# A decoder trunk's mixer: projections dealt in four rounds, gates, then output projections; convolution, rotation and merge read PSUM; a smaller DMA scratch

## Chip, cores and metric

The kernel runs on one core of a Trainium2 chip. The metric is the device time of one execution in microseconds (us), here the median of three runs. TensorE (PE in the profile) does matrix products and writes them to PSUM, which has eight banks of 512 fp32 columns here; VectorE (DVE), ScalarE (ACT) and GpSimd (POOL) do the elementwise work, ACT with its function tables; SyncE (SP) issues the transfers from HBM. Every engine runs its own instructions in a fixed order and waits at semaphores for the others.

## The reference, cut to the mixer

Two layers, each a mixer, a mixture of experts and a per-layer embedding. 512 tokens, width 1024, fp32. The change touches the mixer:

```python
h = _rms_norm(x, norm_mix[i])
z = h @ w_in[i]                                  # 1024 -> 512*5 + 2*1024
q, k, v, cu, cg, ga, gb = jnp.split(z, W_IN_SPLITS, axis=-1)
q = _rope(q.reshape(B, S, N_HEADS, HEAD_DIM))    # 8 heads of 64
k = _rope(k.reshape(B, S, N_HEADS, HEAD_DIM))
v = v.reshape(B, S, N_HEADS, HEAD_DIM)
y_a = _dilated_mixture_attention(q, k, v) @ w_attn_out[i]
# causal depthwise convolution of 31 taps over u = cu * sigmoid(cg), then LayerNorm, silu
y_b = _conformer_conv(cu, cg, w_dw[i], b_dw[i], ln_conv_g[i], ln_conv_b[i]) \
    @ w_conv_out[i] + b_conv_out[i]
merged = jax.nn.sigmoid(ga) * y_a + jax.nn.sigmoid(gb) * y_b
x = x + merged @ w_out[i]
h2 = _rms_norm(x, norm_ffn[i])
x = x + _hier_moe(h2, ...)                       # 32 experts, 2 per token
g_ple = jax.nn.sigmoid(_rms_norm(x, norm_ple[i]) @ w_ple_gate[i])
x = x + g_ple * (p[i] @ w_ple_proj[i])
```

## The kernel before

**Weights and products.** The dense weights come in chunks of 512 KB, in the order of `SEQ_CHUNKS`. `load_chunks` (L207) issues a chunk's transfer on SP, `split_chunks` has ACT round it to `hi` (L225) and POOL form the rest `lo` (L230). A product then takes three passes (`mm3`, L288 to L290). `step_a` makes one tile of z transposed: a chunk of 128 columns against all 512 tokens, 8 x 3 = 24 matmuls into one PSUM bank (`ps_z`). Such a product is called a step here. The chunk names say what a step makes: `cu`, `cg` convolution value and gate (4 each), `q`, `k` (4 pairs of heads), `ga`, `gb` gates of the two branches (8 each), so 32 steps per layer. `v` (values) comes ahead of them in another layout, `ao` are the output projections of both branches, 24 matmuls for each of 8 column tiles (`ps_ya`, `ps_yb`), `wo` the product behind the merge (`ps_wo`).

**Order of a mixer before.** `v`; then four pairs `cu`, `cg`; then four pairs `q`, `k`; then three pairs of gates; then the `ao` projections, with the other five pairs of gates behind the first five of them. All steps write PSUM; ACT or DVE takes the result out. For the convolution DVE writes u = (tanh + 1) * value to SBUF (L514).

**Side work.** Everything that the steps feed lies in three queues: `conv` (the taps, two at a time), `attn` (rotation, and for each pair of heads six score groups with their softmax, transposes and the product with the values), `side` (the last taps of a chunk, LayerNorm and silu). A step calls `adv` four times; each call takes one entry from `conv` and `side`, and in the `q`, `k` and gate steps three from `attn`. So the place in which an entry is written follows from the steps; Tile's scheduler then fixes each engine's order, with `attn` and `side` at high priority.

**Taps.** 31 shifted multiply-adds per chunk (`tap`, L499: acc = u shifted * weight + acc). DVE does 26 of them, ACT with POOL the last five (`ptap`, L505, L506), by the table `KP`.

**Rotation.** ACT copies the product to `raw` (L677) and, in four pieces with the halves of each head exchanged, to `sw` (L679); DVE multiplies by cosine (L588) and sine (L589) and adds (L590) to `s_qk`. The scores (`ps_S`, L603) are PE's; DVE takes minimum and bias (L609), ACT the exponential (L611), DVE the reciprocal and scaling (L621, L625), PE the transposes (`ps_PT`, L637), and `ps_O` (L663) multiplies by the values.

**Memory.** SBUF tiles of 128 x 1024 come from a pool `s4` of 44, tiles of 128 x 512 from `s2` of 12. Expert weights take what `s4` has free (`pump`, L241).

Of the kernel before, what the change touches and what calls it, by code (L numbers as in the profile page):

```python
# [13 lines left out]
OP = mybir.AluOpType  # L14
# [16 lines left out]
# columns of the constant array  # L31
# [5 lines left out]
# columns of the per-layer array of small weights  # L37
# [29 lines left out]
AD = 3, 3, 3  # L67
KP = 5, 5, 5, 5
# [3 lines left out]
RP = "vvv"  # L72
# [6 lines left out]
N4, N2 = 44, 12  # L79


class Pinned:
    """An engine that issues its instructions in the order they are written."""
# [25 lines left out]
class Halved:  # L109
    """n rows of 512 columns, in halves of 256, four to a tile."""  # L110
# [15 lines left out]
class Slots:  # L126
    """Tiles of one size; a slot is free again once its last use is written down."""
# [15 lines left out]
class Rows:  # L143
    """n rows of 512 columns, two to a tile."""
# [11 lines left out]
class Trunk:  # L156
    def __init__(self, ctx, tc, x, pT, wd, wg, wu, wdn, sm, gains, cst, out):
# [16 lines left out]
        self.queues = []  # L174
        # expert weights in the order of their use
# [34 lines left out]
    def split_chunks(self, upto):  # L210
        """The parts of the weights that one pass carries each: rounded, and the rest."""
# [34 lines left out]
    def late_items(self):  # L246
        """Some of the first weights in use come last, into half tiles."""
# [53 lines left out]
    def step_a(self, c, adv=1):  # L301
        """A tile of z^T: a chunk of 128 columns against all tokens."""
# [3 lines left out]
        for k in range(KD):  # L306
            w = slice(k * P, (k + 1) * P)
            self.mm3(ps, ch[:, w], cl[:, w], hh(k), hl(k), k == 0, k == KD - 1)
            if k % 2:
                self.adv(adv)  # L310
# [3 lines left out]
    def step_b(self, c, acc, src, k0, first, last):  # L314
        """Token-layout products: a chunk of 2 x 128 rows against 512 columns."""
        ch, cl = self.take(c)
        for t in range(NT):
# [4 lines left out]
            self.adv(1)  # L322
# [34 lines left out]
    def squares(self, t, junk, h):  # L357
        """Sum of the squares of a half of a token tile."""
# [29 lines left out]
    def split_T(self, t, n, dst):  # L388
        """Transposes of one token tile into the two parts of dst."""
# [14 lines left out]
    def prep(self, t, gain, r, n):  # L404
        """RMSNorm(x) of a token tile."""
# [60 lines left out]
    def mixer(self, l):  # L466
# [9 lines left out]
        # values, in token layout  # L476
# [24 lines left out]
        def ptap(j, s):  # L501
            o, i = acc(j, s), u(j, 0, T - s)
# [6 lines left out]
        for j in range(4):  # L509
            pcu = self.step_a(pos[f"cu{j}"])  # L510
# [3 lines left out]
            v.scalar_tensor_tensor(u(j), th, 1.0, pcu, op0=OP.add, op1=OP.mult)  # L514
# [45 lines left out]
        def silu_part(j):  # L560
# [12 lines left out]
            if j == 3:  # L573
                self.s2.free()  # 1/std
# [11 lines left out]
        def rope(dst, raw, sw):  # L586
            e = [dict(p=nc.gpsimd, v=v)[a] for a in RP]
            e[0].tensor_tensor(dst, raw, self.cc(C_COS, T), op=OP.mult)  # L588
            e[1].tensor_tensor(sw, sw, self.cc(C_SIN, T), op=OP.mult)  # L589
            e[2].tensor_tensor(dst, dst, sw, op=OP.add)  # L590
# [80 lines left out]
        for p in range(4):  # L671
            st["qk", p] = Rows(self.s4, 2, what="qk")
            for i, nm in enumerate(("q", "k")):
                ps = self.step_a(pos[f"{nm}{p}"], adv=AD[0])
                raw, sw = self.s2.get(F32, "raw"), self.s2.get(F32, "sw")
                scale = 0.125 if nm == "q" else 1.0
                act.activation(raw, ps, AF.Copy, scale=scale)  # L677
                for b in range(0, P, 32):
                    act.activation(sw[b:b + 32], ps[b ^ 32:(b ^ 32) + 32], AF.Copy, scale=scale)  # L679
                self.ps.free()  # L680
                attn.append(lambda d=st["qk", p](i), r=raw, w=sw: rope(d, r, w))
# [3 lines left out]
            attn += [dict(u=us, t=tr, n=nm_)[a[0]][int(a[1])] if a != "-" else None for a in ATT.split()]  # L685
# [12 lines left out]
        gates = {}

        def gate(nm, j):  # L700
            ps = self.step_a(pos[f"{nm}{j}"], adv=AD[1])
            g = self.s2.get(F32, nm)
            act.activation(g, ps, AF.Tanh, scale=0.5)
            self.ps.free()
            gates[nm, j] = g

        for j in range(3):
            gate("ga", j)
            gate("gb", j)
        for q in self.queues:  # L710
            self.drain(q)
        self.look, self.ahead = LK[1], 1
        mT = Halved(self.s4, KD, F32R, "mTh"), Halved(self.s4, KD, F32R, "mTl")
        for j in range(8):
# [3 lines left out]
            for s, src in ((0, oT), (1, cv)):  # L718
# [4 lines left out]
            ga, gb = gates.pop(("ga", j)), gates.pop(("gb", j))  # L723
            yb = self.s2.get(F32, "yb")
            v.scalar_tensor_tensor(ga, ga, 1.0, pab[0], op0=OP.add, op1=OP.mult)
            act.activation(yb, pab[1], AF.Identity, bias=self.smt[:, S_BO + j:S_BO + j + 1])
            v.scalar_tensor_tensor(gb, gb, 1.0, yb, op0=OP.add, op1=OP.mult)
            v.tensor_add(ga, ga, gb)
            for h in range(2):
                a = slice(256 * h, 256 * h + 256)  # L730
                act.activation(mT[0].half(j, h), ga[:, a], AF.Copy, scale=0.5)
# [739 lines left out]
```

## Time and profile before

| | before |
|---|---|
| median of three runs | 2046.5 us (2046.15 to 2046.57) |
| span of the profiled execution, first to last instruction | 2042.4 us |
| PE busy | 1885.1 us |
| DVE busy | 984.4 us |
| ACT busy | 580.8 us |
| POOL busy | 419.5 us |
| mean granted clock of PE | 0.966 |

No time of its own is recorded for the profiled execution; its span is 4.1 us below the median. The page cuts the span into 40 slices and gives each engine's busy share in tenths. Further views are asked of the same trace: windows (busy time by stretch), waits (who waited for whom), single tiles, groups of instructions by line, and the timeline. Matmuls overlap in the pipeline, so the time of one (0.39 us) is longer than the distance between two.

### The profile page before, as it was taken

What the parts mean: (1) busy time and instruction counts of PE and PEld (TensorE: products, weight loads), DVE (VectorE), ACT (ScalarE), POOL (GpSimd) and SP (SyncE); (2) the same over time, 40 slices, a digit from 0 to 9 for tenths busy, and PEclk for the clock granted to TensorE, in tenths of its full rate; (3) what the DMA queues carried; (4) which work ended last, traced back from release to release, by engine and by line L of the source; (5) the groups of instructions that cost most, each with busy time, mean ns of one, the idle gap of its engine ahead of it and who ended that gap; (6) DMA issues with size and microseconds to landing.
All of it is one profiled execution on the core that took longest, in us unless ns stands there. A gap on an engine that the chain in (4) does not pass through costs nothing. (4 is left out here: it accounts for less than half of the span.)

```text
span 2042.4 us, 23393 instructions
## 1 busy us (share of the span) xinstructions
PE 1885.1 (92%) x8532; PEld 1120.8 (55%) x8532; DVE 984.4 (48%) x2171; ACT 580.8 (28%) x1097; POOL 419.5 (21%) x211
## 2 busy tenths in 40 slices
PE   6948999999999998999989589999999999989998
PEld 5835588854444344444777356888544444444446
DVE  5799751462333223223659997325532332233246
ACT  4235542321110112111634354423211111111135
POOL 4443452401000001000435353424010000000011
PEclk9978999999999999999999789999999999999999
DMA  5201133579999699896231012254899996999941
GB/s 215 70 31 42 42 124 121 198 268 371 390 395 409 261 409 399 321 347 272 86 109 64 32 32 72 93 194 147 315 371 381 409 408 264 409 356 349 362 193 42
DMA packets 133319, 478.59 MB, mean 234 GB/s; under 512 B 14800, under 2 KB 15312, under 8 KB 133200
## 3 DMA queue, kind: packets, MB, share of 16 engines
q1 hardware_dynamic: 133200, 477.04, 62.2%
q8 instruction: 70, 1.15, 0.2%
q14 instruction: 49, 0.40, 0.1%
HBM read 474.89 MB, written 2.10 MB: 234 GB/s over the span
## 5 line engine op out<-in xcount | busy, mean ns | idle before, releaser
L230 POOL TENSOR_TENSOR s_lo<-s_raw,s_hi 128x1024 fp32r<-128x1024 f32 x114 | 290.6, 2565 | 766.1 <-ACT s_hi L225 411.7
L1021 PE MATMUL ps_u<-s_w,s_xg 128*64 128x512 f32 x1024 | 266.8, 596 | 0.0
L1021 PE MATMUL ps_g<-s_w,s_xg 128*64 128x512 f32 x1024 | 241.9, 607 | 6.9 <-DVEq L1206 6.5
L1051 PE MATMUL ps_y<-s_w,s_hT 128*64 128x512 f32 x1024 | 241.1, 595 | 1.4 <-ACT s_hT L1040 1.4
L290 PE MATMUL ps_z<-s_hTh,s_lo 128*128 128x512 f32 x512 | 205.5, 401 | 1.2 <-POOL s_lo L230 1.2
L289 PE MATMUL ps_z<-s_hTl,s_hi 128*128 128x512 f32 x512 | 205.4, 401 | 0.0
L288 PE MATMUL ps_z<-s_hTh,s_hi 128*128 128x512 f32 x512 | 205.1, 400 | 0.0
L499 DVE SCALAR_TENSOR_TENSOR s_acc<-s_u,smt,s_acc 128x503 f32<-128x503 f32 (+17 forms) x200 | 203.2, 1038 | 2.1
L1030 DVE SCALAR_TENSOR_TENSOR s_h<-s_h,ps_g 128x512 f32<-128x512 f32 x32 | 21.9, 686 | 292.9 <-ACT s_h L1029 292.9
L1021 PEld LDWEIGHTS ps_u<-s_w,s_xg 128*64 128x64 f32 x1024 | 78.5, 137 | 144.0 <-issue 136.1
L1051 PEld LDWEIGHTS ps_y<-s_w,s_hT 128*64 128x64 f32 x1024 | 77.2, 137 | 146.3 <-issue 129.2
L1074 DVE TENSOR_TENSOR s_x<-s_x,ps_c 128x512 f32<-128x512 f32 x144 | 95.3, 684 | 128.0 <-PE ps_c L1071 127.2
L897 PE MATMUL ps_xg<-s_OH,s_xh 128*128 128x256 f32 x512 | 138.7, 306 | 19.7 <-ACT s_xg L993 17.6
L1040 ACT ACTIVATE s_hT<-ps_hT 128x512 f32<-128x512 f32 x32 | 19.1, 597 | 415.8 <-PE ps_hT L1038 368.3
L1021 PEld LDWEIGHTS ps_g<-s_w,s_xg 128*64 128x64 f32 x1024 | 69.5, 137 | 123.0 <-issue 75.7
L897 PE MATMUL ps_xg<-s_OH,s_xl 128*128 128x256 f32 x512 | 132.7, 292 | 0.0
L897 PEld LDWEIGHTS ps_xg<-s_OH,s_xh 128*128 128x128 f32 x512 | 99.3, 195 | 56.8 <-ACT s_xg L993 38.1
L225 ACT ACTIVATE s_hi<-s_raw 128x1024 fp32r<-128x1024 f32 x120 | 123.3, 1052 | 4.0 <-POOL s_lo L230 3.5
L1138 POOL TENSOR_TENSOR s_pTl<-s_pT,s_pTh 128x1024 fp32r<-128x1024 f32 x2 | 4.7, 2368 | 532.3 <-ACT s_pTh L1137 266.3
L897 PEld LDWEIGHTS ps_xg<-s_OH,s_xl 128*128 128x128 f32 x512 | 99.6, 195 | 22.8 <-issue 22.7
L290 PEld LDWEIGHTS ps_z<-s_hTh,s_lo 128*128 128x128 f32 x512 | 98.4, 192 | 24.8 <-issue 3.5
L289 PEld LDWEIGHTS ps_z<-s_hTl,s_hi 128*128 128x128 f32 x512 | 98.7, 193 | 24.1 <-issue 3.9
(250 smaller groups left out, 2928.3 us busy)
## 6 DMA issues: line engine op xcount, KB each, us to landing
s_w<-wu SPq DMA_DIRECT2D x256, 512.0 KB, 9.5
s_w<-wdn SPq DMA_DIRECT2D x256, 512.0 KB, 10.2
s_w<-wg SPq DMA_DIRECT2D x248, 512.0 KB, 10.1
s_raw<-wd SPq DMA_DIRECT2D x124, 512.0 KB, 3.5
s_w<-wg SPq DMA_DIRECT2D x16, 256.0 KB, 7.5
s_x<-x SPq DMA_DIRECT2D x4, 512.0 KB, 9.1
out<-s_n SPq DMA_DIRECT2D x8, 256.0 KB, 2.0
s_gain<-gains SPq DMA_DIRECT2D x3, 512.0 KB, 3.8
```

The source lines that it names most:

```text
L225: nc.scalar.activation(hi, raw, AF.Copy)
L230: nc.gpsimd.tensor_tensor(lo, raw, hi.bitcast(F32), op=OP.subtract)
L288: mm(out, lh, rh, start=start, stop=False)
L289: mm(out, lh, rl, start=False, stop=False)
L290: mm(out, ll, rh, start=False, stop=stop)
L499: v.scalar_tensor_tensor(o, i, w, o, op0=OP.mult, op1=OP.add)
L897: self.nc.tensor.matmul(ps, self.nh[o][t][:, k * P:(k + 1) * P], oh[:, t * GS:(t + 1) * GS], start=t == 0 and o == 0, stop=t == NT - 1 and ...
L1021: pe.matmul(ps[64 * e:64 * e + 64], xg[h // 2][:, s:s + CAP], self.half_item((l, w, 2 * p + e, h), k), start=h == 0 and k == 0, stop=h == ...
L1030: v.scalar_tensor_tensor(t, t, 1.0, pg, op0=OP.add, op1=OP.mult)
L1040: act.activation(o, ps, AF.Copy)
L1051: pe.matmul(ps[n][64 * e:64 * e + 64], h_[:, f * P + e * CAP:f * P + (e + 1) * CAP], self.item_tile[l, "d", 2 * p + e, f][:, n * T:(n + 1) ...
L1074: v.tensor_add(xs, xs, ps)
```

## The change

The chunks, and with them the steps, are dealt in four rounds: each round p is `cu`, `cg`, `q`, `k`, `ga`, `gb` of number p. After the rounds come the other four pairs of gates, and then all eight `ao` projections in a row. `adv` now runs `attn` at one entry per call, and at two in every fourth (`AD`). The gated value u stays in the PSUM bank of its product, and the taps read it there; the fourth chunk's 31 taps are all DVE's (`KP`). The rotation multiplies the product in PSUM: sine first, ACT exchanges the halves from SBUF, then cosine in PSUM and the sum (the sign of the sine table moves with it). The merge of the branches is done in the PSUM banks of the two projections, convolution first. All gates lie in `s4`, and their tiles are held until the merge. The scratch that is set aside for dynamic DMA is 4096 bytes per partition, and `s4` has 47 tiles. Comments are removed, which moves the line numbers.

```diff
-SEQ_CHUNKS = (["v0", "v1", "v2", "v3", "cu0", "cg0", "cu1", "cg1", "cu2", "cg2", "cu3", "cg3",
-               "q0", "k0", "q1", "k1", "q2", "k2", "q3", "k3",
-               "ga0", "gb0", "ga1", "gb1", "ga2", "gb2"]
-              + [s for j in range(8) for s in ([f"ao{j}"] + ([f"ga{j + 3}", f"gb{j + 3}"] if j + 3 < 8 else []))]
+SEQ_CHUNKS = ([f"v{i}" for i in range(4)]
+              + [f"{n}{p}" for p in range(4) for n in ("cu", "cg", "q", "k", "ga", "gb")]
+              + [f"{n}{j}" for j in range(4, 8) for n in ("ga", "gb")]
+              + [f"ao{j}" for j in range(8)]
...
-AD = 3, 3, 3
-KP = 5, 5, 5, 5
+AD = 1, 1, 1, 2
+KP = 5, 5, 5, 0
...
-N4, N2 = 44, 12
+N4, N2 = 47, 12
+SCRATCH = 4096
...
-    def adv(self, n=1):
+    def adv(self):
+        self.adv_n += 1
         for i, q in enumerate(self.queues):
-            for _ in range(n if i == 1 else 1):
+            for _ in range(AD[self.adv_n % len(AD)] if i == 1 else 1):
...
         def tap(j, s):
-            o, i = acc(j, s), u(j, 0, T - s)
+            o, i = acc(j, s), u[j][:, :T - s]
...
-        for j in range(4):
-            pcu = self.step_a(pos[f"cu{j}"])
+        def conv_in(j):
+            u[j] = pcu = self.step_a(pos[f"cu{j}"])
             pcg = self.step_a(pos[f"cg{j}"])
             th = self.s2.get(F32, "th")
             act.activation(th, pcg, AF.Tanh, scale=0.5)
-            v.scalar_tensor_tensor(u(j), th, 1.0, pcu, op0=OP.add, op1=OP.mult)
-            self.ps.free(2)
+            v.scalar_tensor_tensor(pcu, th, 1.0, pcu, op0=OP.add, op1=OP.mult)
+            self.ps.free()
...
-        def rope(dst, raw, sw):
-            e = [dict(p=nc.gpsimd, v=v)[a] for a in RP]
-            e[0].tensor_tensor(dst, raw, self.cc(C_COS, T), op=OP.mult)
-            e[1].tensor_tensor(sw, sw, self.cc(C_SIN, T), op=OP.mult)
-            e[2].tensor_tensor(dst, dst, sw, op=OP.add)
+        def rope(dst, ps, scale):
+
+            a, sw = self.s2.get(F32, "raw"), self.s2.get(F32, "sw")
+            v.tensor_tensor(a, ps, self.cc(C_SIN, T), op=OP.mult)
+            for b in range(0, P, 32):
+                act.activation(sw[b:b + 32], a[b ^ 32:(b ^ 32) + 32], AF.Copy, scale=scale)
+            v.scalar_tensor_tensor(ps, ps, scale, self.cc(C_COS, T), op0=OP.mult, op1=OP.mult)
+            v.tensor_tensor(dst, ps, sw, op=OP.add)
...
-        for p in range(4):
+        def pair(p):
             st["qk", p] = Rows(self.s4, 2, what="qk")
             for i, nm in enumerate(("q", "k")):
-                ps = self.step_a(pos[f"{nm}{p}"], adv=AD[0])
...
-                attn.append(lambda d=st["qk", p](i), r=raw, w=sw: rope(d, r, w))
+                ps = self.step_a(pos[f"{nm}{p}"])
+                with self.tc.high_priority(HP):
+                    rope(st["qk", p](i), ps, 0.125 if nm == "q" else 1.0)
...
+        for p in range(4):
+            conv_in(p)
+            pair(p)
+            gate_pair(p)
+            if p == 3:
+                conv.append(norm)
         self.scale_router()
...
+        for j in range(4, 8):
+            gate_pair(j)
+        for s in self.hT:
+            s.free()
         for q in self.queues:
             self.drain(q)
...
-            for s, src in ((0, oT), (1, cv)):
+            for s, src in ((1, cv), (0, oT)):
...
-            ga, gb = gates.pop(("ga", j)), gates.pop(("gb", j))
-            yb = self.s2.get(F32, "yb")
-            v.scalar_tensor_tensor(ga, ga, 1.0, pab[0], op0=OP.add, op1=OP.mult)
-            act.activation(yb, pab[1], AF.Identity, bias=self.smt[:, S_BO + j:S_BO + j + 1])
-            v.scalar_tensor_tensor(gb, gb, 1.0, yb, op0=OP.add, op1=OP.mult)
-            v.tensor_add(ga, ga, gb)
+            g = gates.pop(0)
+            ga, gb = g[:, :T], g[:, T:]
+            act.activation(pab[1], pab[1], AF.Identity, bias=self.smt[:, S_BO + j:S_BO + j + 1])
+            v.scalar_tensor_tensor(gb, gb, 1.0, pab[1], op0=OP.add, op1=OP.mult)
+            v.scalar_tensor_tensor(pab[0], ga, 1.0, pab[0], op0=OP.add, op1=OP.mult)
+            v.tensor_tensor(pab[0], pab[0], gb, op=OP.add)
...
-            if j + 3 < 8:
-                gate("ga", j + 3)
-                gate("gb", j + 3)
...
-    nc = bacc.Bacc("TRN2", target_bir_lowering=False, num_devices=1)
+    nc = bacc.Bacc("TRN2", target_bir_lowering=False, num_devices=1, dynamic_dma_scratch_size=SCRATCH)
```

How this moves the instructions is seen at two places. First PE's order in layer 0 where the first scores stand. Before, it is behind eleven whole steps (`ps_z_841` is `q1`, the eleventh, `ps_z_924` is `k1`; `s_qk_734` holds the first pair's rotated queries and keys):

```order
L289 MATMUL ps_z_841<-s_hTl_107,s_hi_634 128x512
L290 MATMUL ps_z_841<-s_hTh_103,s_lo_635 128x512
L603 MATMUL ps_S_875<-s_qk_734 128x128
L603 MATMUL ps_S_902<-s_qk_734 128x384
L603 MATMUL ps_S_875<-s_qk_734 128x256
L288 MATMUL ps_z_924<-s_hTh_100,s_hi_685 128x512
```

Now it is behind five steps and the first matmul of the sixth (`ps_z_580` is `ga0`, `ps_z_620` is `gb0`; `s_qk_476` holds the first pair):

```order
L290 MATMUL ps_z_580<-s_hTl_107,s_hi_411 128x512
L291 MATMUL ps_z_580<-s_hTh_103,s_lo_412 128x512
L289 MATMUL ps_z_620<-s_hTh_100,s_hi_442 128x512
L609 MATMUL ps_S_635<-s_qk_476 128x128
L609 MATMUL ps_S_663<-s_qk_476 128x384
L609 MATMUL ps_S_635<-s_qk_476 128x256
L290 MATMUL ps_z_620<-s_hTl_104,s_hi_442 128x512
```

The scores have moved ahead of six steps; a later score group now stands at the end of each step, where before several stood in one. Second, DVE's order at the first pair's rotation. Before, the rotation follows all 26 taps of the first two chunks (`s_u_405` holds chunks 0 and 1, `s_u_406` chunks 2 and 3, `s_acc` the sums; `s_c` are the tables):

```order
L499 SCALAR_TENSOR_TENSOR s_acc_407<-s_u_405,smt,s_acc_407 128x488
L499 SCALAR_TENSOR_TENSOR s_acc_407<-s_u_405,smt,s_acc_407 128x487
L589 TENSOR_TENSOR s_sw_773<-s_sw_773,s_c_94 128x512
L497 TENSOR_SCALAR s_acc_408<-s_u_406,smt 128x512
L588 TENSOR_TENSOR s_qk_734<-s_raw_772,s_c_93 128x512
L499 SCALAR_TENSOR_TENSOR s_acc_408<-s_u_406,smt,s_acc_408 128x511
L588 TENSOR_TENSOR s_qk_734<-s_raw_827,s_c_93 128x512
L590 TENSOR_TENSOR s_qk_734<-s_qk_734,s_sw_773 128x512
```

Now it stands among the taps of chunk 0, which read the bank `ps_z_417` (`cu0`); `ps_z_531` is `k0`, and the last row is the first score group's minimum:

```order
L501 SCALAR_TENSOR_TENSOR s_acc_405<-ps_z_417,smt,s_acc_405 128x503
L591 TENSOR_TENSOR s_raw_564<-ps_z_531,s_c_94 128x512
L594 SCALAR_TENSOR_TENSOR ps_z_531<-ps_z_531,s_c_93 128x512
L501 SCALAR_TENSOR_TENSOR s_acc_405<-ps_z_417,smt,s_acc_405 128x502
L501 SCALAR_TENSOR_TENSOR s_acc_405<-ps_z_417,smt,s_acc_405 128x501
L501 SCALAR_TENSOR_TENSOR s_acc_405<-ps_z_417,smt,s_acc_405 128x500
L595 TENSOR_TENSOR s_qk_476<-ps_z_531,s_sw_565 128x512
L501 SCALAR_TENSOR_TENSOR s_acc_405<-ps_z_417,smt,s_acc_405 128x499
L501 SCALAR_TENSOR_TENSOR s_acc_405<-ps_z_417,smt,s_acc_405 128x498
L501 SCALAR_TENSOR_TENSOR s_acc_405<-ps_z_417,smt,s_acc_405 128x497
L615 ISA s_S_636,m_639<-ps_S_635,s_c_93 128x128
```

Ahead of the first pair's last rotation instruction stand 14 convolution instructions now, where there were 52 taps and more; three further taps follow before the first minimum.

More of the change, by code (lines that the diff above doesn't have):

```diff
@@ L71 @@
 NRM = "vvv"
-RP = "vvv"
 AH = 4
@@ L173, in __init__ @@
         self.loaded = self.split_n = 0
-        self.queues = []
+        self.queues, self.adv_n = [], 0
         self.items, self.item_tile, self.item_next, self.ring = [], {}, 0, 0
@@ L309, in step_a @@
             if k % 2:
-                self.adv(adv)
+                self.adv()
         self.done(c)
@@ L488, in mixer @@
         self.scale_small(l)
-        u, acc = Rows(self.s4, 4, what="u"), Rows(self.s4, 4, what="acc")
+        acc = Rows(self.s4, 4, what="acc")
+        u = {}
         def tap(j, s):
-            o, i = acc(j, s), u(j, 0, T - s)
+            o, i = acc(j, s), u[j][:, :T - s]
             w = self.wh[:, j * CK + CK - 1 - s:j * CK + CK - s]
@@ L536, in mean_part @@
             nc.tensor.matmul(pm, self.cc(C_ONE, P), sums[0], start=True, stop=True)
-            self.s2.free()
+            sq = sums[0]
             for j in range(4):
                 v.tensor_sub(acc(j), acc(j), pm)
-                act.activation(u(j), acc(j), AF.Square)
+                t = sq if j == 0 else self.s2.get(F32, "sq")
+                act.activation(t, acc(j), AF.Square)
                 if j:
-                    v.tensor_add(u(0), u(0), u(j))
+                    v.tensor_add(sq, sq, t)
+                    self.s2.free()
             self.ps.free()
@@ L548, in var_part @@
             pv = self.ps.get(F32, "var")
-            nc.tensor.matmul(pv, self.cc(C_ONE, P), u(0), start=True, stop=True)
+            nc.tensor.matmul(pv, self.cc(C_ONE, P), sums[0], start=True, stop=True)
             a, y, t = (self.s2.get(F32, "ln") for _ in range(3))
@@ L684, in mixer @@
             tr = [lambda p=p, q=q: trans(p, q) for q in range(6)]
-            attn += [dict(u=us, t=tr, n=nm_)[a[0]][int(a[1])] if a != "-" else None for a in ATT.split()]
+            attn.extend(dict(u=us, t=tr, n=nm_)[a[0]][int(a[1])] if a != "-" else None for a in ATT.split())
             def last(p=p):
@@ L693, in mixer, with gate_pair @@
             attn.append(last)
-        self.scale_router()
[L698 to L709, printed above, removed]
+        gates = []
+        def gate_pair(j):
+            g = self.s4.get(F32, "g")
+            for i, nm in enumerate(("ga", "gb")):
+                ps = self.step_a(pos[f"{nm}{j}"])
+                act.activation(g[:, i * T:(i + 1) * T], ps, AF.Tanh, scale=0.5)
+                self.ps.free()
+            gates.append(g)
+        for p in range(4):
[4 more added lines that the diff above has]
+                conv.append(norm)
+        self.scale_router()
+        for j in range(4, 8):
+            gate_pair(j)
+        for s in self.hT:
+            s.free()
         for q in self.queues:
@@ L722, in mixer @@
             self.done(c)
[L723 to L728 removed]
+            g = gates.pop(0)
[4 more added lines that the diff above has]
+            v.tensor_tensor(pab[0], pab[0], gb, op=OP.add)
             for h in range(2):
                 a = slice(256 * h, 256 * h + 256)
[L731 to L732 removed]
+                act.activation(mT[0].half(j, h), pab[0][:, a], AF.Copy, scale=0.5)
+                v.scalar_tensor_tensor(mT[1].half(j, h), pab[0][:, a], 0.5, mT[0].half(j, h).bitcast(F32),
                                        op0=OP.mult, op1=OP.subtract)
             self.ps.free(2)
[L735 to L741 removed]
+            self.s4.free()
             self.pump(RING[0])
@@ L1398, in constants @@
     c[:, C_COS:C_COS + T] = np.cos(ang.astype(np.float64))
-    c[:, C_SIN:C_SIN + T] = np.sin(ang.astype(np.float64)) * np.where(i % HD < HD // 2, -1.0, 1.0)[:, None]
+    c[:, C_SIN:C_SIN + T] = np.sin(ang.astype(np.float64)) * np.where(i % HD < HD // 2, 1.0, -1.0)[:, None]
     c[:, C_BASE:C_BASE + 32] = np.arange(32) * CAP
```

25 lines of the change are left out of this document (6 added, 19 removed).

## The prediction

> **What bounds the kernel now.** I read the page first, for the engine whose share is highest and for where it has holes.
>
> ```profile
> PE 1885.1 (92%) x8532; PEld 1120.8 (55%) x8532; DVE 984.4 (48%) x2171; ACT 580.8 (28%) x1097; POOL 419.5 (21%) x211
> PE   6948999999999998999989589999999999989998
> DVE  5799751462333223223659997325532332233246
> ```
>
> TensorE (PE) is busy for 92% of the span. Each slice is 51 us; PE's digits drop to 4 in slice 3 and to 5 in slice 23, once in each layer, and exactly there VectorE (DVE) stands at 9. These are the mixers, the stages that the change rewrites. Next the windows view, cut at the mixer's first input product, at the hole, and at the first output projection (columns: stretch and its length, busy PE, weight loads, DVE, ACT, POOL, then PE's granted clock, DMA share and GB/s).
>
> ```profile
> 50.00:110.04 60.04, 60.03 (x265) 49.36 (x263) 47.49 (x47) 23.02 (x34) 30.94 (x13) 1.00 0.20 63
> 110.04:135.20 25.16, 0.00 (x1) 0.00 (x1) 24.91 (x23) 0.53 (x1) 15.19 (x9) 0.58 0.16 59
> 135.20:267.30 132.10, 121.76 (x476) 77.03 (x477) 113.19 (x238) 72.58 (x163) 44.96 (x30) 0.92 0.15 48
> 267.30:366.30 99.00, 98.43 (x435) 81.11 (x434) 30.64 (x47) 34.24 (x53) 36.48 (x15) 1.00 0.41 142
> 50.00:267.30 217.30, 181.80 (x741) 126.39 (x740) 185.60 (x306) 96.13 (x197) 91.09 (x51) 0.91 0.16 54
> 1058.80:1277.60 218.80, 183.35 (x742) 127.42 (x741) 184.85 (x306) 97.33 (x198) 93.06 (x51) 0.90 0.16 53
> ```
>
> PE stands still for 25 us while DVE works without a pause, and it loses 35.5 us of 217.3 in all; layer 1 repeats this. From 267.3 to 366.3 it is the other way round: PE is full and DVE has 30.6 us of work in 99. So the mixer is bound by DVE first and by PE later. The waits of PE name what it waited for (sum, times, longest): layer 0, then layer 1.
>
> ```profile
> PE ps_S L603 <- DVE s_qk L590: 27.1, 2, 25.2
> PE ps_PT L637 <- DVE den L621: 4.7, 2, 4.4
> PE ps_PT L637 <- DVE s_S L625: 3.5, 4, 1.8
> PE ps_S L603 <- DVE s_qk L590: 27.7, 3, 25.1
> ```
>
> The first scores wait for the rotation of the first pair, which stands in DVE's order behind the 52 convolution taps of two chunks (the order excerpts above). The 16 gate products, which wait for nothing of DVE's, come too late to fill the hole.
>
> **What PE alone would need.** First matmuls of the mixer and of the stage behind it, both layers, and the pitch of an input product:
>
> ```profile
> L288 PE MATMUL ps_z<-s_hTh,s_hi x256: 387/389/793, 50.0 to 349.3; 128*128 128x512 f32 x128
> L288 PE MATMUL ps_wo<-s_hi,s_mTh x32: 389/389/389, 366.3 to 387.3; 128*128 128x512 f32 x32
> L288 PE MATMUL ps_z<-s_hTh,s_hi x256: 387/389/793, 1058.9 to 1359.5; 128*128 128x512 f32 x128
> L288 PE MATMUL ps_wo<-s_hi,s_mTh x32: 389/389/390, 1376.5 to 1397.5; 128*128 128x512 f32 x32
> 50.03 0.39 PE L288 MATMUL ps_z<-s_hTh,s_hi 128*128 128x512 f32 x1
> 81.77 0.39 PE L290 MATMUL ps_z<-s_hTh,s_lo 128*128 128x512 f32 x1
> ```
>
> The mixer from cu0 to wo0 takes 316.3 us in layer 0 and 317.6 in layer 1. The last two rows are the first and the 141st matmul of an unbroken run: 31.74 / 140 = 0.2267 us each. A step (24 matmuls) is 5.44 us; 32 input steps are 174.1 us and 8 output projections 43.5 us. The attention's own matmuls, layer 0 (scores, transposes, values; only the second number is read), and the same six score matmuls at two clocks:
>
> ```profile
> 50.00:267.30 217.30, 26.97 (x64) 10.68 (x64) 14.73 (x32) 0.91 0.16 54
> 50.00:267.30 217.30, 18.72 (x80) 9.80 (x80) 5.31 (x16) 9.97 (x32) 0.91 0.16 54
> 50.00:267.30 217.30, 13.89 (x64) 6.31 (x64) 2.74 (x4) 2.39 (x4) 0.91 0.16 54
> 135.20 2.92 PE L603 MATMUL ps_S<-s_qk 64*128 64x128 f32 x6 [25.16 <-DVE s_qk L590]
> 166.20 1.56 PE L603 MATMUL ps_S<-s_qk 64*128 64x128 f32 x6
> ```
>
> They sum to 59.6 us with two small matmuls (about 2) to come, but part of it ran slowly: after the hole the six took 2.92 us against 1.56 later. The clock was 0.92 over 132.1 us, some 10 us of full speed missing, not all of it in these rows. So attention costs PE between 51 and 62 us; I take 54. PE's floor is 174.1 + 43.5 + 54 = 271.6 us, and what can be won is 316.3 - 271.6 = 44.7 and 317.6 - 271.6 = 46.0, together **90.7 us**. Cross-check: 35.5 of idle time plus 0.6 in the output window leave 8.6 for the slow clock.
>
> **The change part by part.** *The four rounds.* They add and remove no input product. A round is six steps, 32.7 us, plus a pair's attention. The first scores now stand after five steps and one matmul, at about 50.0 + 27.4 = 77.4 us. Ahead of them DVE has, from the gated value (cu0 and cg0 done at 60.9, tanh 0.6), 14 convolution instructions and six for the rotation, about 14 us: the rotation is done near 76. Later, each score group stands one step before its transposes; between them lie DVE's minimum, ACT's exponential and DVE's scaling, some 3 us without queueing, in 5.4 to 7 us. So DVE is just ahead at the start and then waits for PE.
>
> *Convolution input left in PSUM.* The taps are DVE's largest item:
>
> ```profile
> L499 DVE SCALAR_TENSOR_TENSOR s_acc<-s_u,smt,s_acc 128x503 f32<-128x503 f32 (+17 forms) x200 | 203.2, 1038 | 2.1
> L499 DVE SCALAR_TENSOR_TENSOR s_acc<-s_u,smt,s_acc 128x511 f32<-128x511 f32 x4 | 7.1, 1771 | 0.0
> L499 DVE SCALAR_TENSOR_TENSOR s_acc<-s_u,smt,s_acc 128x490 f32<-128x490 f32 x4 | 2.9, 716 | 0.0
> L609 DVE CUSTOM_DVE_ANT_0 s_S<-ps_S,s_c 128x512 f32<-128x512 f32 x8 | 5.5, 683 | 3.1 <-PE ps_S L603 3.1
> L514 DVE SCALAR_TENSOR_TENSOR s_u<-s_th,ps_z 128x512 f32<-128x512 f32 x4 | 2.7, 680 | 21.0 <-ACT s_th L513 21.0
> ```
>
> From SBUF alone a tap costs 0.72 to 1.77 us by its place, 1.04 on average. Instructions with one PSUM operand cost 0.68 in the same stretches, with POOL busy for a third of the time. A tap from PSUM isn't in this trace: bounds 0.68 and 1.77; I take 0.68, the row with the same operands. DVE's work before the projections is then 185.6 - 100 x 1.038 + 105 x 0.68 = 153 us (the fourth chunk takes five more taps from ACT and POOL). The place for it runs from 62 to the floor's first projection at 50 + 174.1 + 54 = 278 us: 216 us. At 1.04 the work is 191 us and still fits. So DVE leaves the path, and the price of a tap scarcely shows. The Trainium skill ("VectorE: DVE Perf Modes", section "Rules for kernel authors") advises to copy PSUM data to SBUF first where many operations follow; by it this edit gives speed away. No such loss shows in the two PSUM rows: the measurement decides, and the sum stays.
>
> *Rotation and merge from PSUM.* Each rotation loses ACT's copy of the product (eight per layer); each projection's bias and sums are done in place. The same number of DVE instructions, 0.68 each, about 3 us per projection beside 5.4 of PE: nothing on the path. In the projections the split of the next weights now queues on ACT behind the bias activation, which waits for PE's half projection; POOL then takes 2.6 us. One such split may be late by a microsecond.
>
> *Loads.* SP's chunk loads follow the new order; one chunk per 5.4 us against a median landing of 3.5 us keeps them hidden. Gates move into the large tiles, and three more of these exist for expert weights.
>
> ```profile
> q1 hardware_dynamic: 133200, 477.04, 62.2%
> s_w<-wdn SPq DMA_DIRECT2D x256, 512.0 KB, 10.2
> s_raw<-wd SPq DMA_DIRECT2D x124, 512.0 KB, 3.5
> 750.00:775.00 25.00, 25.00 (x117) 8.98 (x116) 3.75 (x7) 3.97 (x6) 0.25 (x1) 1.00 1.03 410
> ```
>
> In the expert stage PE is full while the transfers run at 410 GB/s, so three more tiles can win only little there: 0, with 4 us either way kept for the range. The smaller DMA scratch I cost at nothing, since the weight loads go through SP's hardware queue. The Trainium skill ("SBUF — State Buffer", section "SBUF size: 192, 224, or 256?") calls this area the descriptor ring of software DMA; no run here shows what it holds.
>
> *New waits.* In the stretch where DVE had caught up, 205 to 265 us, PE still lost:
>
> ```profile
> 217.21 0.30 PE L637 MATMUL ps_PT<-c,s_S 128*128 128x128 f32 x1 [0.34 <-DVE den L621]
> 234.43 1.53 PE L603 MATMUL ps_S<-s_qk 64*128 64x128 f32 x6 [1.96 <-DVE s_qk L590]
> ```
>
> That is 2.3 us in 60, or 6 us over the 165 us in which attention will be spread. With DVE less loaded I take 5 per layer, bounds 0 and 10.
>
> **Sum.** Span 2042.4 - 90.7 + 2 x 5 = 1961.7 us. The median of the runs, 2046.5, lies 4.1 above the profiled span; with that the time is **1966 us**, 3.9% less. Its own range: 1956 with no new wait, 1976 with ten per layer; with attention at 51 or 62, 1960 or 1982.
>
> **Rivals.** (1) *The hand-offs take the place of the old wait.* PE's order is fixed; 24 score groups per layer each have to pass DVE, ACT and DVE within a step, and ACT also carries taps and weight splits. If each group is late by a further microsecond, that is 24 per layer: 1966 + 48 = 2014. For it: the 4.7 and 3.5 us of waits above. Against: they fell where DVE had a backlog.
> (2) *DVE stays the bound.* In 110 to 267 us DVE was idle for 19 of 157 us, 12%, though it was the bound. The mixer ends later than before once DVE's work / 0.88 exceeds 216 + 45 = 261 us, that is from 230 us of work, a tap price of 1.41 us. At the row of 1.77 it is 153 + 105 x 1.09 = 267, or 304 us, 43 later per layer: 2046 + 86 = 2132, **slower**. Against it stand the two PSUM rows.
> (3) *The floor is lower or the experts gain.* Attention at 51, no wait and 4 us from the tiles: 1966 - 6 - 10 - 4 = 1946.
> (4) *The change doesn't even out the work*: PE idles elsewhere, for example at the projections because the last pair is late. The hole stays as large and the time within 0.2% (about what a measurement of this kernel can tell from no change): 2046. Against: behind the last values product stand more than four gate steps, 22 us.
>
> **How the numbers follow.** Forecast 0.73, (1) 0.14, (2) 0.03, (3) 0.07, (4) 0.03. The range takes the forecast's own bounds, attention at 62, most of (3) and the lower half of (1): 1948 to 1994. Faster by over 0.2%: 0.95 (forecast, (1), (3) and a part of the rest); within it: 0.02; slower: 0.03.
>
> **What would show it.** In the changed profile: PE's mixer slices at 9 with no wait over 2 us on the scores; PE's clock 1.00 throughout; cu0 to wo0 at 272 to 282 us per layer; taps near 0.68 us; DVE near 70% in the mixer, its idle time released by PE; the expert stage as long as before. It is wrong if PE still waits for DVE over 10 us per layer, if taps cost over 1 us, or if the expert stage changes by more than 5 us.

## The result and the profile after

The changed kernel takes **1953.0 us** (median of four runs, 1948.6 to 1953.9) where the kernel before took 2046.3 beside it: 0.9543 of the time, 95% interval 0.9528 to 0.9558, or 93 us less. The profiled execution is the fastest of the four, with a span of 1946.8 us and a granted clock of 0.989 (before: 2042.4 and 0.966). In the page the busy shares and three rows of the 40 slices (48.7 us each) answer to those of before.

```profile
PE 1850.1 (95%) x8532; PEld 1103.9 (57%) x8532; DVE 915.8 (47%) x2181; ACT 568.2 (29%) x1071; POOL 377.2 (19%) x201
PE   5999999999999998999989999998999999989997
DVE  5577753652234223224658777537341334133156
PEclk9999999999999999999999999999999999999999
```

Before, the clock row dipped at both holes:

```profile
PEclk9978999999999999999999789999999999999999
```

Both holes of PE (the 4 and the 5) are gone, and DVE's 9s with them: its work is spread over five slices in each layer, of 5 to 7 in layer 0 and of 5 to 8 in layer 1. TensorE does the same 8532 matmuls in 35 us less busy time, 21 of them in the mixers, where nothing runs at a lower clock any more. The marks of the mixer (first input product, first output projection) and the windows view between them, layer 0 and layer 1, and up to the last input product of layer 0:

```profile
L289 PE MATMUL ps_z<-s_hTh,s_hi x256: 387/389/504, 51.6 to 278.9; 128*128 128x512 f32 x128
L289 PE MATMUL ps_wo<-s_hi,s_mTh x32: 388/389/397, 324.5 to 346.2; 128*128 128x512 f32 x32
...
51.60:324.50 272.90, 270.36 (x1173) 202.64 (x1173) 185.65 (x357) 124.50 (x237) 107.50 (x61) 1.00 0.28 94
1013.60:1286.50 272.90, 270.37 (x1174) 202.68 (x1173) 185.77 (x357) 125.45 (x238) 108.42 (x61) 1.00 0.28 93
51.60:279.50 227.90, 226.43 (x981) 166.61 (x981) 164.42 (x321) 108.63 (x209) 95.62 (x56) 1.00 0.21 69
```

A mixer takes 272.9 us in either layer, PE busy for 270.4 of it at clock 1.00; DVE works 164 of the first 228 us, 72%. What PE still waits for in layer 0 (sum, times, longest):

```profile
PE ps_PT L643 <- DVE s_S L631: 1.4, 2, 1.0
PE ps_yb L291 <- POOL s_lo L230: 1.1, 1, 1.1
PE ps_wo L290 <- POOL s_lo L230: 0.3, 1, 0.3
```

No score waits. The span fell by 95.6 us: 43.4 and 44.7 in the two mixers, 9.1 in the expert and embedding stages behind them, less 1.6 by which the first mixer started later.

### The profile page after: what moved, and what is told of

Its sections match the earlier page's. It is cut to its first block, busy times and chain, and to the rows that moved or that the text cites. A ratio compares the mean times of both kernels' runs of the same rounds, so it can differ in the third digit from the quotient of the medians.

```text
span 1946.8 us, 23363 instructions
## 1 busy us (share of the span) xinstructions
PE 1850.1 (95%) x8532; PEld 1103.9 (57%) x8532; DVE 915.8 (47%) x2181; ACT 568.2 (29%) x1071; POOL 377.2 (19%) x201
## 5 line engine op out<-in xcount | busy, mean ns | idle before, releaser
L230 POOL TENSOR_TENSOR s_lo<-s_raw,s_hi 128x1024 fp32r<-128x1024 f32 x114 | 272.3, 2401 | 763.4 <-ACT s_hi L225 507.3
L1025 PE MATMUL ps_u<-s_w,s_xg 128*64 128x512 f32 x1024 | 260.0, 595 | 0.0
L291 PE MATMUL ps_z<-s_hTh,s_lo 128*128 128x512 f32 x512 | 199.7, 390 | 0.0
L501 DVE SCALAR_TENSOR_TENSOR s_acc<-ps_z,smt,s_acc 128x511 f32<-128x511 f32 (+27 forms) x210 | 153.8, 732 | 4.2
L901 PE MATMUL ps_xg<-s_OH,s_xh 128*128 128x256 f32 x512 | 135.6, 302 | 19.7 <-ACT s_xg L997 17.5
L289 PEld LDWEIGHTS ps_z<-s_hTh,s_hi 128*128 128x128 f32 x512 | 96.1, 188 | 21.3 <-issue 1.0
```

What stands on the lines that cost most here:

```text
L230: nc.gpsimd.tensor_tensor(lo, raw, hi.bitcast(F32), op=OP.subtract)
L289: mm(out, lh, rh, start=start, stop=False)
L291: mm(out, ll, rh, start=False, stop=stop)
L501: v.scalar_tensor_tensor(o, i, w, o, op0=OP.mult, op1=OP.add)
L901: self.nc.tensor.matmul(ps, self.nh[o][t][:, k * P:(k + 1) * P], oh[:, t * GS:(t + 1) * GS], start=t == 0 and o == 0, stop=t == NT - 1 and ...
L1025: pe.matmul(ps[64 * e:64 * e + 64], xg[h // 2][:, s:s + CAP], self.half_item((l, w, 2 * p + e, h), k), start=h == 0 and k == 0, stop=h == ...
```

## The experiments

Twelve further kernels were run. Each is the changed kernel with the edit shown, except that e4_before47 edits the kernel before, and e5_sbuf_nopool and e6_sbuf_ct1 stand on top of e2_u_sbuf. The diffs are shortened, and some of their lines give the edit in words. Times are medians; the ratio is to the kernel before on the same chip, with its 95% interval; the other columns are from each kernel's profiled execution: the two mixers (cu0 to wo0), then wo0 of layer 0 to cu0 of layer 1, and wo0 of layer 1 to the end.

| run | us | ratio (95%) | mixers | stages behind | clock |
|---|---|---|---|---|---|
| before | 2046.3 | 1 | 316.3, 317.6 | 692.6, 665.9 | 0.966 |
| after | 1953.0 | 0.9543 (0.9528–0.9558) | 272.9, 272.9 | 689.1, 660.3 | 0.989 |
| e1_old_order | 2025.4 | 0.9899 (0.9885–0.9914) | 308.2, 308.9 | 691.4, 661.0 | 0.967 |
| e2_u_sbuf | 2007.8 | 0.9806 (0.9792–0.9821) | 299.7, 301.3 | 692.0, 666.5 | 0.972 |
| e3_n44 | 1958.5 | 0.9575 (0.9562–0.9587) | 272.9, 272.9 | 694.1, 666.6 | 0.988 |
| e4_before47 | 2041.9 | 0.9974 (0.9966–0.9983) | 318.0, 319.5 | 687.0, 665.9 | 0.964 |
| e5_sbuf_nopool | 1957.9 | 0.9564 (0.9550–0.9579) | 273.2, 273.2 | 688.3, 666.7 | 0.987 |
| e6_sbuf_ct1 | 2052.3 | 1.0024 (1.0013–1.0036) | 321.6, 322.8 | 691.1, 665.4 | 0.958 |
| e7_rope_sbuf | 1966.4 | 0.9611 (0.9596–0.9625) | 281.8, 283.0 | 689.0, 660.3 | 0.986 |
| e8_ahead2 | 1966.2 | 0.9608 (0.9595–0.9622) | 271.6, 271.4 | 697.4, 672.5 | 0.985 |
| e9_ahead_reset | 1953.1 | 0.9548 (0.9535–0.9561) | 273.2, 271.5 | 692.5, 661.4 | 0.984 |
| e10_order_alone | 2022.4 | 0.9895 (0.9880–0.9910) | 307.5, 305.9 | 691.1, 665.7 | 0.968 |
| e11_ad3 | 1996.5 | 0.9765 (0.9742–0.9787) | 294.6, 296.0 | 689.8, 661.2 | 0.969 |
| e12_kp5 | 1954.8 | 0.9548 (0.9534–0.9563) | 273.5, 273.6 | 692.5, 662.2 | 0.985 |

### e1_old_order: the PSUM edits without the rounds

```diff
-  {n}{p} for p in range(4) for n in ("cu", "cg", "q", "k", "ga", "gb"), then gates 4-7, then ao0-7
+  cu/cg 0-3, q/k 0-3, ga/gb 0-2, then ao{j} with ga/gb{j+3} behind it
-AD = 1, 1, 1, 2;  KP = 5, 5, 5, 0
+AD = 3, 3, 3, 3;  KP = 5, 5, 5, 5
```

> The changed kernel with the steps put back into the old order (value and gate of all four convolution chunks first, then queries and keys, then three gate pairs, the other five between the output projections, and ACT and POOL taking five taps of every chunk again); convolution input, rotation and merge still read PSUM, 47 large tiles. Theory 'order': the first scores still stand behind 52 taps; at 0.73 us instead of 1.04 these are 38 us instead of 54, so the wait of 25 us at the first scores shrinks to about 9 and does not go; cu0 to wo0 about 300 us per layer, time about 2010 (2000 to 2030). Rival 'taps': cheaper taps alone lift DVE off the path in the old order too: no wait over 3 us, cu0 to wo0 near 275, time within 10 us of 1953.

PE's longest waits in layer 0's mixer, and its window:

```profile
PE ps_PT L644 <- DVE s_S L632: 16.7, 4, 9.5
PE ps_S L610 <- DVE s_qk L596: 3.3, 1, 3.3
...
50.40:358.60 308.20, 284.24 (x1173) 209.71 (x1172) 173.25 (x352) 127.37 (x242) 113.00 (x66) 0.94 0.24 80
```

The time is in the range of "order", 20 us below the kernel before. But the wait at the first scores shrank to 3.3 us, further than the 9 expected, and most of the hole moved on to the transposes (9.5 us at once), which wait for a softmax queued in DVE: ten taps, 6.5 us from 152.8 us on, stand ahead of its minimum. Cheaper taps move the hole and take some of it away; they don't close it. This kernel also deals the attention three pieces at a time, as the kernel before does; the old order at the new pace was not run.

### e2_u_sbuf: the rounds, taps from SBUF

```diff
-u = {};  taps read u[j][:, :T - s] (the PSUM tile of the value product)
+u = Rows(self.s4, 4, what="u");  taps read u(j, 0, T - s)
-v.scalar_tensor_tensor(pcu, th, 1.0, pcu, ...)
+v.scalar_tensor_tensor(u(j), th, 1.0, pcu, ...)
```

> The changed kernel, but the gated convolution input is written to SBUF and the 105 taps per layer read it there; order of the rounds, rotation, merge and tiles as in the changed kernel. Theory 'order': a tap costs about 1.04 us again, DVE's work in the mixer grows by 105 x 0.31 = 32 us to some 185 of 216 us, and PE hardly notices: cu0 to wo0 273 to 279 us per layer, time 1953 to 1966. Rival 'taps': the reading from PSUM is needed: cu0 to wo0 over 288 us, time over 1983.

Window and waits of layer 0's mixer:

```profile
49.90:349.60 299.70, 279.97 (x1174) 208.14 (x1173) 211.51 (x357) 124.19 (x237) 111.09 (x61) 0.97 0.26 86
...
PE ps_PT L643 <- DVE den L627: 7.7, 2, 3.9
PE ps_PT L643 <- DVE s_S L631: 7.4, 3, 4.7
PE ps_S L609 <- DVE s_qk L595: 3.5, 4, 3.0
```

"Order" fell: 55 us slower than the changed kernel. DVE has 211.5 us of work in 299.7, so on the sum it has time to spare; still PE waits 19.7 us, 1.1 of it for a weight split and the rest for the rotation and the softmax, which stand among the taps in DVE's order. And the loss is larger than the waits: 26.8 us, of which 9.6 are PE's own matmuls running longer (280.0 busy against 270.4) at a clock of 0.97.

What a tap costs, by kernel: duration in ns, minimum/median/maximum, in the view of one line. First the kernel before, then this run, then the changed kernel.

```profile
L499 DVE SCALAR_TENSOR_TENSOR s_acc<-s_u,smt,s_acc x200: 701/732/2875, 63.1 to 1230.0; 128x496 f32<-128x496 f32 x8, 128x494 f32<-128x494 f32 x8, 128x492 f32<-128x492 f32 x8, 128x490 f32<-128x490 f32 x6
```
```profile
L501 DVE SCALAR_TENSOR_TENSOR s_acc<-s_u,smt,s_acc x210: 701/737/2978, 63.0 to 1250.2; 128x511 f32<-128x511 f32 x4, 128x509 f32<-128x509 f32 x4, 128x507 f32<-128x507 f32 x4, 128x505 f32<-128x505 f32 x4
```
```profile
L501 DVE SCALAR_TENSOR_TENSOR s_acc<-ps_z,smt,s_acc x210: 703/732/750, 65.0 to 1192.1; 128x511 f32<-128x511 f32 x4, 128x509 f32<-128x509 f32 x4, 128x507 f32<-128x507 f32 x4, 128x505 f32<-128x505 f32 x4
```

Median and minimum are the same from SBUF and from PSUM. Only the longest differ, 2.9 and 3.0 us against 0.75, and with them the mean. The timeline of this run shows one such place, DVE's taps and POOL's weight split beside them (start, duration):

```profile
123.33 5.86 DVE L501 SCALAR_TENSOR_TENSOR s_acc<-s_u,smt,s_acc 128x503 f32<-128x503 f32 x5
...
123.96 2.37 POOL L230 TENSOR_TENSOR s_lo<-s_raw,s_hi 128x1024 fp32r<-128x1024 f32 x1 [12.32 <-ACT s_hi L225]
```

Five taps at the median would be 3.7 us; they took 2.2 longer, about the split's 2.37. In the changed kernel four taps run beside such splits in their usual time:

```profile
122.88 3.03 DVE L501 SCALAR_TENSOR_TENSOR s_acc<-ps_z,smt,s_acc 128x497 f32<-128x497 f32 x4
...
123.40 4.93 POOL L230 TENSOR_TENSOR s_lo<-s_raw,s_hi 128x1024 fp32r<-128x1024 f32 x2 [7.42 <-ACT s_hi L225]
```

### e5_sbuf_nopool: the same with POOL kept still

```diff
+plain = nm[:2] in ("cu", "cg", "ga", "gb", "ao") or nm[0] in "qk"
-nc.gpsimd.tensor_tensor(lo, raw, hi.bitcast(F32), op=OP.subtract)
+if plain: self.hl[c] = hi, self.zero
```

> The kernel of the run before (rounds, gated convolution input in SBUF), but POOL no longer computes the low part of the mixer's input and output projection weights: these chunks take one tile of zeros as their low part (this part of the computation is left out; TensorE, the taps and the loads stay; 46 large tiles beside the tile of zeros). Theory 'POOL holds up DVE': a tap from two SBUF operands takes 0.70 to 0.74 us when POOL is still, and the mean of 1.00 comes from the few that stand beside POOL's 2.4 us instructions; now the mean is under 0.80, PE's waits fall from 20 us to under 6 per layer, cu0 to wo0 272 to 278. Rival 'SBUF operands are dearer in themselves': the mean tap stays near 1.0 and cu0 to wo0 near 300.

The kernel leaves out a part of the computation: the low part of these weights is never formed, and a tile of zeros stands for it.

The taps, and the first mixer's window:

```profile
L512 DVE SCALAR_TENSOR_TENSOR s_acc<-s_u,smt,s_acc x210: 706/735/752, 71.1 to 1196.4; 128x511 f32<-128x511 f32 x4, 128x509 f32<-128x509 f32 x4, 128x507 f32<-128x507 f32 x4, 128x505 f32<-128x505 f32 x4
...
57.80:331.00 273.20, 273.20 (x1174) 202.76 (x1173) 173.96 (x357) 124.63 (x237) 24.80 (x26) 1.00 0.27 89
```

"POOL holds up DVE" held in full. From SBUF, with POOL busy 24.8 us instead of 111, no tap is over 0.752 us, PE waits for nothing, and the mixer takes 273.2 us. What PSUM gives the taps is not speed but freedom from POOL. Not every instruction of DVE is freed by the change: the softmax's scaling works from SBUF to SBUF in the changed kernel too, and there it takes 0.28 to 2.31 us (L631, median 0.48); one piece of 256 columns takes 1.92 us from 129.70 us on, beside a split that starts at 129.07. It is also the instruction for which PE still waits 1.4 us in a layer.

### e6_sbuf_ct1: taps dealt more thinly

```diff
-CT, CG = 2, 4
+CT, CG = 1, 4
```

> The kernel with the rounds and the gated convolution input in SBUF, with the taps dealt one at a time instead of two between pairs of matmul groups, nothing else. A mean tap stays near 1.0 us. Theory 'bursts': PE's waits (20 us of 300 in a layer's mixer) come from taps being dealt faster than DVE can do them beside the softmax, 8 us of taps per step of 5.4 us; at 4 us per step the waits on the scores' and softmax's DVE work fall under 6 us per layer, though the convolution's end may now be late by some us; cu0 to wo0 275 to 288, time 1958 to 1984. Rival 'sum': DVE's whole work is what is too much; cu0 to wo0 stays over 294, time over 1996.

PE's waits in layer 0's mixer, and the 67 us from the last input product to wo0:

```profile
PE ps_S L609 <- DVE s_qk L595: 14.0, 4, 5.3
PE ps_yb L289 <- ACT s_cv L573: 11.7, 1, 11.7
PE ps_var L553 <- DVE s_sum L545: 4.9, 1, 4.9
...
305.00:372.00 67.00, 49.39 (x200) 38.32 (x200) 42.61 (x71) 23.59 (x40) 11.85 (x5) 0.87 0.45 154
```

"Bursts" fell: the scores still wait for the rotation (14.0 us), and the convolution now ends after the last gate, so that its norm stands in front of the projections. By time the rival was nearer, but it did not foresee this late end, which costs 16.6 us of waits in layer 0 (11.7 and 4.9) and so makes the run slower than the kernel before.

### e7_rope_sbuf: the rotation as before

```diff
-v.tensor_tensor(a, ps, sin);  act: sw <- a (halves swapped);  v: ps <- ps * scale * cos;  v: dst <- ps + sw
+act: raw <- ps;  act: sw <- ps (halves swapped);  v: dst <- raw * cos;  v: sw <- sw * sin;  v: dst <- dst + sw
```

> The changed kernel with the rotation done as before (ACT copies the product and its swapped halves to SBUF, DVE's three instructions work in SBUF). Theory 'taps alone': the rotation is 24 instructions per layer against 105 taps, its way out of PSUM is worth nothing: within 5 us of the changed kernel, 1950 to 1958, first scores at the same place. Rival 'the rotation counts too': its three instructions stretch beside POOL and hold up the scores, over 1963.

The rotation's last instruction here and in the changed kernel (groups: count, busy us, mean ns, idle before), and this run's first wait:

```profile
L597 DVE TENSOR_TENSOR s_qk<-s_qk,s_sw 128x512 f32<-128x512 f32 x16 | 22.8, 1425 | 0.0
...
PE ps_S L610 <- DVE s_qk L597: 5.0, 3, 4.4
```
```profile
L595 DVE TENSOR_TENSOR s_qk<-ps_z,s_sw 128x512 f32<-128x512 f32 x16 | 11.0, 687 | 1.4 <-ACT s_sw L593 1.2
```

"Taps alone" fell: 13 us more. From SBUF an addition takes 1.43 us on average instead of 0.69, and the scores wait for it. As with the taps only the long ones differ: the median from SBUF is 0.69 us too, the longest 2.87.

### e10_order_alone: neither read from PSUM

The edits of e2_u_sbuf and e7_rope_sbuf together.

> The four rounds with nothing of the mixer's convolution and rotation read from PSUM: gated input in SBUF, rotation as before (merge and 47 tiles as in the changed kernel). Theory 'the rotation adds': taps at 1.0 us and the rotation's three instructions at 1.0 to 1.4, and PE waits for both; 12 us more than the run with only the gated input in SBUF, about 2020 (2014 to 2032). Rival 'one queue': once DVE is late the rotation hides behind the taps, within 6 us of 2008.

```profile
PE ps_S L610 <- DVE s_qk L597: 16.5, 4, 7.8
```

In the waits of layer 0's mixer the scores lead with 16.5 us: "the rotation adds", by 15 us. So the rounds alone, with the tiles, bring 23.5 us (ratio 0.9895), the PSUM edits in the old order 20.4 (0.9899), of which the tiles are about 4 in each (next); both together bring 93. Without the tiles these are 19.5, 16.5 and 89: some 53 us of the gain come only when both are there. "The rounds" here means the new order together with the new pace of the attention. The merge from PSUM is in both of these kernels, and no run prices it alone.

### e3_n44 and e4_before47: the tiles

```diff
-N4, N2 = 47, 12
+N4, N2 = 44, 12
```
```diff
-N4, N2 = 44, 12
+N4, N2 = 47, 12
+SCRATCH = 4096
```

> The changed kernel with 44 large tiles as before, nothing else. Theory 'tiles': the 9 us that the expert and embedding stages gained come from the three more tiles for weights: wo0 of layer 0 to cu0 of layer 1 is 692 to 693 us again and wo0 of layer 1 to the end 665 to 666, time about 1962. Rival 'not the tiles' (the clock, or the order in which the stage starts): both stretches stay at 689 and 660 within 1.5 us, time within 2 us of the changed kernel's.

> The kernel before with 47 large tiles and the smaller DMA scratch, nothing else. Theory 'tiles': 9 us less, about 2037, with wo0 to cu0 near 689 and wo0 to the end near 660. Rival 'not the tiles': 2046 within 2 us, both stretches at 692 and 666 within 1.5 us.

The up products of layer 0's experts, in the groups of the stage, with 44 tiles (e3_n44) and with 47 (changed kernel):

```profile
L1025 PE MATMUL ps_u<-s_w,s_xg 128*64 128x512 f32 x512 | 133.4, 596 | 0.0
```
```profile
L1025 PE MATMUL ps_u<-s_w,s_xg 128*64 128x512 f32 x512 | 130.0, 595 | 0.0
```

The tiles bring 4 us (2045.8 to 2041.9) to 5 (1958.5 to 1953.0; by the two ratios 6.5), about half of "tiles". The row of the kernel before reads 133.4 as well, and that of e4_before47 130.0; whether those 3.4 us per layer are a wait for weights no row says. The other half lies within the spread: with 47 or 46 tiles, and e8_ahead2 aside, the two stages together took 1349.3 to 1358.5 us in the profiled executions, and the changed kernel's 1349.4 is at their short end.

### e8_ahead2 and e9_ahead_reset: the late split

```diff
-self.look, self.ahead = LK[1], 1
+self.look, self.ahead = LK[1], 2
```
```diff
 for j in range(8):
     c = pos[f"ao{j}"]
+    self.ahead = 2 if j < 6 else 1
```

> The changed kernel, but in the output projections the weights are split two chunks ahead instead of one. Theory 'late split': PE's waits for POOL's low part (1.1 us at the second projection and 0.3 at the first merged one, per layer) go, 2 to 3 us less in all, about 1950. Rival: the waits go but ACT's and POOL's work then meets the merge, no change within 1.5 us.

> The changed kernel, with the weights split two chunks ahead in the first six output projections only, and one ahead again from the seventh on. Theory 'tiles held': what the run with two ahead throughout lost (10 us and more behind the projections) came from the tiles that the early splits kept from the expert weights in the routing stage; now the mixer keeps its 1.4 us per layer (cu0 to wo0 271.5) and the stages behind are as in the changed kernel, 687 to 692 and 660 to 666 us; time 1948 to 1954. Rival 'ACT and POOL': their order in the projections and the routing is what cost it; time over 1960 again.

With two ahead throughout, the mixers lose their late split (271.6 and 271.4 us), but both stages behind grow, by 8 and 12 us, and the time with them. Already in the first 80 us from wo0 on, PE is busy for less; the windows of this run and of the changed kernel:

```profile
323.10:403.10 80.00, 68.29 (x353) 53.66 (x353) 42.05 (x194) 22.21 (x44) 23.76 (x10) 0.96 0.63 207
```
```profile
324.50:404.50 80.00, 74.58 (x387) 56.28 (x386) 42.00 (x203) 24.91 (x50) 26.11 (x11) 0.96 0.62 213
```

With the reset the stages are back in their usual span, so the loss did come from splitting further ahead behind the projections. Whether tiles or the queues of ACT and POOL carry it, the two runs don't tell. The late split is gone in both layers, but only layer 1 gains by it (271.5 us). In layer 0 PE's matmuls run 1.4 us longer at a clock of 0.99, and the mixer takes 273.2. No gain shows in the time: 1953.1.

### e11_ad3 and e12_kp5: the pace, and the fourth chunk

```diff
-AD = 1, 1, 1, 2
+AD = 3, 3, 3, 3
```
```diff
-KP = 5, 5, 5, 0
+KP = 5, 5, 5, 5
```

> The changed kernel with the attention's pieces dealt three at a time, as in the kernel before, instead of one or two. Theory 'pace matters': a score group and its transposes then stand a third of a step apart, 1.8 us, where minimum, exponential and scaling take about 3: PE waits over 15 us per layer in the mixer, time over 1980. Rival 'DVE is ahead': within 8 us of 1953.

> The changed kernel with five taps of the fourth chunk on ACT and POOL again instead of DVE. Theory 'not on the path': four gate pairs, 43.5 us, stand behind it: within 3 us of the changed kernel, 1950 to 1957. Rival: the five POOL additions, one after another behind the weight splits, make the convolution's end late: PE waits at the first output projection, over 1958.

In e11_ad3, layer 0's mixer, its first transposes, and the clock around them:

```profile
50.10:344.70 294.60, 285.44 (x1173) 211.49 (x1172) 175.24 (x357) 122.96 (x237) 107.12 (x61) 0.94 0.26 87
...
81.14 0.30 PE L643 MATMUL ps_PT<-c,s_S 128*128 128x128 f32 x1 [1.98 <-DVE s_S L631]
...
80.10:83.10 3.00, 1.96 (x6) 0.86 (x7) 3.00 (x10) 0.82 (x4) 0.00 (x0) 0.97 0.00 0
83.10:86.10 3.00, 3.00 (x9) 1.90 (x10) 0.43 (x2) 0.18 (x1) 0.00 (x0) 0.50 0.00 0
86.10:89.10 3.00, 3.00 (x8) 2.32 (x8) 2.96 (x11) 3.00 (x9) 0.42 (x1) 0.50 0.00 0
89.10:92.10 3.00, 3.00 (x13) 1.86 (x12) 0.81 (x5) 0.63 (x3) 1.95 (x1) 0.89 0.07 10
```

"Pace matters", though not as it was put: the time is over 1980 (1996.5), but PE's waits sum to only 9.2 us in 294.6, 6.7 more than in the changed kernel. The other 15.0 of the 21.7 us lost per mixer are PE busy for longer, 285.4 us against 270.4, at a clock of 0.94. The five taps of e12_kp5 are not on the path: within 2 us.

## Why the prediction held, and where it did not

The forecast was 1966, the time is 1953.0: 13 us lower, inside the range, and on the side that was given 0.95. It is nearer to rival (3), 1946, whose terms came, a lower attention and few waits in part, the gain from the tiles in full. The hand-offs of rival (1) are not late by a microsecond each: in the changed kernel two of them in a layer wait, for 1.4 us together. The forecast's picture of the change is the one that the runs show: both holes go, PE becomes the bound, PE's clock stays at 1.00 in the mixer, DVE stands at 72%. Its terms:

- **Floor and new waits.** The mixers gave 88.1 us where 80.7 were summed. New waits are 2.5 us per layer up to wo0 instead of 5. With them taken off 272.9, and 217.6 for the products, attention cost 52.8 instead of 54. That is 7.4 us together. The late split was foreseen at 1 us and measured 1.1; the first scores came 27.6 us after cu0, foreseen at 27.4.
- **Experts.** The sum had 0, with 4 us either way, and "wrong if the expert stage changes by more than 5". It changed by 9.1 in the profiled execution. The term was mis-sized: three more tiles are worth 4 to 5 us, and the rest lies within the spread of 1349.3 to 1358.5 us between the profiled executions; the four times of the changed kernel alone lie 5.3 us apart.
- **Around the span.** The first mixer started 1.6 us later. The 4.1 us over the span were 2.3 too many: in nearly every run listed here 1.7 to 1.9 us lie around the span, and the rest was the profiled execution of before being a short one. The changed kernel's was a short one too, by 4.5 us. All together, -14.9 for the span, -2.3 and +4.5 make -12.7.
- **The price of a tap** was taken as 0.68 us and is 0.73; DVE's work came to 164 us instead of 153, of which the taps' price makes 5. Here the step that failed is not the price but the conclusion drawn beside it: "At 1.04 the work is 191 us and still fits. So DVE leaves the path, and the price of a tap scarcely shows." e2_u_sbuf is this very case: DVE has 190 us of work ahead of the projections, as foreseen, and the time is 55 us longer. That the wrong conclusion did the number no harm is luck: the taps came out near the 0.68 that was taken, not near the 1.04 that was thought as good. DVE works through its queue in order, and what PE waits for stands in it behind the taps; that a sum fits into the stretch says nothing of when a single instruction gets its turn. Rival (2) put the point from which DVE decides at 1.41 us per tap; the taps from SBUF, far below that, already cost 27 us per layer.
- **Rotation and merge from PSUM** were "nothing on the path". With the rotation put back, the time is 13 us longer (e7_rope_sbuf); the merge was not tried.
- **The pace of the attention** had no term of its own. The prediction used it ("in 5.4 to 7 us" between scores and transposes), but did not price it: three pieces at a time cost 43 us (e11_ad3).

On the order against the PSUM edits the prediction took the order as the cause and the edits as free. The runs show neither alone: 16 and 20 us without the tiles, and more than half of the gain only together. How the rounds' share divides between order and pace is open: in the new order the old pace costs 43 us, and the new pace in the old order was not run.

Two rules of the Trainium skill bear on this. "SBUF — State Buffer", section "SBUF: two separate sides", says that a DVE instruction with two SBUF inputs and a GpSimd instruction that reads SBUF lock each other out, the later one waiting for the whole of the other. The rows agree: taps of up to 2.98 us beside 2.4 us splits, 0.75 at most once one operand comes from PSUM or POOL's splits are left out. "VectorE: DVE Perf Modes", section "Rules for kernel authors", advises a copy to SBUF where many operations follow on PSUM data; here, with 105 of them per layer beside a busy POOL, leaving the data in PSUM is 55 us faster, and the measurement decides.

## What to carry to other kernels

When an engine that works in order is busy for three quarters of a stretch, don't ask whether its sum fits but what is queued ahead of the instruction that the bound engine waits for. Look at minimum, median and maximum of a costly group before taking its mean as a price: a median of 0.73 beside a maximum of 2.9 was contention here, and it went when one operand was moved to PSUM. Price edits together as well as apart: two groups of edits that bring under 20 us each brought 89 together.

## What the runs showed of the hardware

A short wait of PE can cost more than itself. In e11_ad3 a wait of 1.98 us, with small attention products around it, was followed by a clock of 0.50 from 83.1 to 89.1 us; in all PE's busy time grew by 15.0 us beside 6.7 us of added waits, in e2_u_sbuf by 9.6 beside 17.2.

In the mixers of all these kernels every wait of over 3 us (3.06 to 25.23) was followed by a clock of 0.50. After shorter waits it sometimes was and sometimes wasn't. In e9_ahead_reset the same wait of 1.03 us was followed by 0.50 in layer 0 and by 1.00 in layer 1; in the kernel before, the same wait of 1.96 us was followed by 1.00 in layer 0 and by 0.50 in layer 1. So the length of a short wait doesn't decide alone; what else does, these runs don't show. The Trainium skill ("TensorE: Matmul & The Clock Gate", section "HAM oscillation — how this bites in real kernels") warns of idle gaps above about 3.4 us; here gaps of 1.03 and 1.98 us were enough in some places.
